# Spreading an expert's closing steps over two stages of the next expert

## The chip, the cores and the metric

The kernel runs on one core of a Trainium2 chip. The metric is the device time of one execution in microseconds (us). Three runs of the kernel before took between 1490.14 and 1492.38 us, with a median of 1491.45 us.

## The reference, cut to what matters

Two decoder layers on 256 tokens of width 1024, all in float32. The first layer ends in a dense SwiGLU, the second in eight SwiGLU experts of width 3584, of which each token takes two. The change is in the experts alone:

```python
def swiglu(x, w_gate, w_up, w_down):
    return (jax.nn.silu(x @ w_gate) * (x @ w_up)) @ w_down
...
y = y * w_buf[:, None].astype(y.dtype)
out = jax.ops.segment_sum(y, tok_buf, num_segments=T)
```

An expert's tokens are gathered, put through its three weight matrices, weighted by their gate and added back to the rows of the tokens that they came from.

## The kernel before, in words

`experts` (L980) works through eight jobs, one for each expert. The first is expert 0, the others come in a fixed order of their ranks by token count (`TURN`, L42). A job is **wide** (128 token slots) or **narrow** (64 slots); jobs 1, 3 and 5 are narrow. Each job runs in two chunks of 1792 hidden columns (c = 0 and 1), and each chunk in two stages, called gate and up here:

- **gate**: eight pieces of the gate weights (k = 0 to 7, L1169) come by DMA from SP's queue. ACT copies each half of a piece to a rounded high part `wh` (L177), DVE subtracts to get the low part `wl` (L180), and PE multiplies the gathered tokens `xg` by both (L1053). There are eight buffers for `wh` and eight for `wl`, so ACT and DVE can be at most eight halves ahead of PE. In a narrow job the eighth piece is multiplied as it came, without splitting.
- **up**: the same for the up weights (L1202). Before it ACT applies Silu to the gate's products (L1194); after it DVE multiplies the two (L1217).

The pieces of the down matrix of the chunk before are split and multiplied in between (`more`, `down`), some before the Silu, some behind the up pieces. A wide half costs PE six matmuls (four with `wh`, two with `wl`), a narrow one four, while ACT and DVE do the same work for both.

Around these loops a list `side` holds small steps. One step is taken behind each piece, and those left over run behind the last piece. Four kinds of step go on it:

- `to_features` (L1125): PE transposes the finished chunk, ACT and DVE split it into `hT`.
- `combine` (L1088): two parts for an expert whose last down product is done. Part i has ACT copy half i of the result out of PSUM into `ys` (L1092) and DVE make its low part (L1093); then, for two blocks of tokens, two matmuls with the one-hot matrix `DT` send the rows to their tokens and one DVE instruction adds them to `x_tok` (L1099).
- `transposed` (L1033): DVE writes a one-hot block `D` (L999), PE transposes it, DVE copies it to `DT` (L1040). It serves the combine of the same job later.
- `dispatch` (L1003): DVE writes the one-hot `D` of the next one or two jobs, at once; then eight steps, each with four matmuls into a PSUM bank of tag "a" and the ACT copies into `xg` (L1023).

`side` is taken in gate by the transposes, the two combine parts and `transposed`, all in chunk 1 of the next job. In up of chunk 1 of jobs 0, 2, 4 and 6 it is taken by the eight dispatch steps; in the other up stages it is empty. `D` and `ys` share one tag, "ys", whose pool has one buffer, so each of these tiles waits until the one before it has been read.

The order on each engine is laid down when the kernel is built, by a list scheduler: among the instructions whose inputs its own timing says are ready, it takes the one that comes first in the program. An instruction far down the program can therefore stand early on an engine that would otherwise be idle. `pin` keeps marked instructions in program order among themselves; `fence` keeps later `wl` behind a dispatch's `D`.

Of the kernel before, what the change touches and what calls it, by code (L numbers as in the profile page):

```python
# [9 lines left out]
F32 = mybir.dt.float32  # L10
F32R = mybir.dt.float32r
I32 = mybir.dt.int32
AF = mybir.ActivationFunctionType
ALU = mybir.AluOpType
# [3 lines left out]
P = 128  # L18
T = 256
NB = 2  # L20
D = 1024
# [44 lines left out]
def trunk(ctx, tc, x, positions, w_in, conv_w, a_log, dt_bias, gdn_norm_w, lam_q1, lam_k1, lam_q2, lam_k2,  # L66
# [3 lines left out]
    V, S, G, PE = nc.vector, nc.scalar, nc.gpsimd, nc.tensor  # L70
# [9 lines left out]
    def nm(s):  # L80
        cnt[0] += 1
        return f"{s}_{cnt[0]}"


    def bank(tag):
        return ps.tile([P, 512], F32, tag=tag, name=nm("ps_" + tag))
# [8 lines left out]
    def pin(ins):  # L95
        return tc.keep_in_program_order(ins)

    def mm(o, lhsT, rhs, start, stop):
        return PE.matmul(o, lhsT, rhs, start=start, stop=stop, skip_group_check=True)  # L99
# [880 lines left out]
    def experts(xs, jobs, mp, ring2, rest, first):  # L980
# [13 lines left out]
        def slots(Dt, job, twice=False):  # L994

            _, where, _, narrow = job
            w = 64 if narrow else P
            m = 2 if narrow and twice else 1
            return V.tensor_tensor(Dt.rearrange("p b (m s) -> p b m s", s=w),  # L999
                                   io1[:, 0:w].unsqueeze(1).unsqueeze(1).broadcast_to([P, NB, m, w]),  # L1000
                                   where.unsqueeze(3).broadcast_to([P, NB, m, w]), op=ALU.is_equal)

        def dispatch(group, early=False):  # L1003

            ws = [64 if job[3] else P for job in group]
            W = sum(ws)
            Dt = mp.tile([P, NB, W], F32R, tag="ys", name=nm("D"))
            for j, job in enumerate(group):
                fence[0] = pin(slots(Dt[:, :, sum(ws[:j]):sum(ws[:j + 1])], job))
            xgs = [xg_tile(job[3]) for job in group]  # L1010

            def part(k):
                pt = bank("ab"[k % 2] if early else "a")
                for c in range(2):
                    for b in range(NB):
                        mm(pt[:, c * W:(c + 1) * W], xs[b][:, c, k * P:(k + 1) * P], Dt[:, b], c == 0 and b == 0,
                           c == 1 and b == 1)
                for j, xg in enumerate(xgs):
                    i = pt[:, 0:2 * W].rearrange("p (c s) -> p c s", s=W)[:, :, sum(ws[:j]):sum(ws[:j + 1])]
                    if early and k % 2:  # L1020
                        fence[0] = pin(V.tensor_copy(xg[:, k], i))
                    else:
                        S.activation(xg[:, k], i, AF.Copy)  # L1023

            return xgs, [lambda k=k: part(k) for k in range(KD)]
# [5 lines left out]
            return x_  # L1031

        def transposed(n):  # L1033
            Dt = mp.tile([P, NB, P], F32R, tag="ys", name=nm("D"))
            slots(Dt, jobs[n], True)
            DT = mp.tile([P, NB, P], F32R, tag=f"DT{n % 2}", name=nm("DT"), bufs=1)
            pt = bank("a")
            for b in range(NB):
                PE.transpose(pt[:, b * P:(b + 1) * P], Dt[:, b].bitcast(F32), ident)
            V.tensor_copy(DT.rearrange("p b t -> p (b t)"), pt[:, 0:NB * P])  # L1040
            return DT
# [44 lines left out]
                                   k == K - 1 and w is wl)  # L1086

        def combine(n, py, DT):  # L1088
            def part(i):
                ys = mp.tile([P, 2, 512], F32R, tag="ys", name=nm("ys"))  # L1090
                yh, yl = ys[:, 0], ys[:, 1]
                S.activation(yh, py[i], AF.Copy)  # L1092
                V.tensor_tensor(yl, py[i], yh.bitcast(F32), op=ALU.subtract)  # L1093
                for b in range(NB):
                    pt = bank("a")
                    mm(pt, DT[:, b], yh, True, False)
                    mm(pt, DT[:, b], yl, False, True)
                    o = x_tok[:, b, i * 512:(i + 1) * 512]
                    V.scalar_tensor_tensor(o, pt, jobs[n][2][:, b], o, op0=ALU.mult, op1=ALU.add)  # L1099

            return [lambda i=i: part(i) for i in range(2)]

        regs = {}

# [39 lines left out]
        def gu_banks():  # L1144
            return [bank(t)[:, 0:BANK] for t in ("mm", "mm", "gd", "gd")]

        groups = [[0], [1, 2], [3, 4], [5, 6], [7]] if NARROW and rest else [[n] for n in range(NE)]
        pend = None
        side = []
        tiles, steps = dispatch([jobs[n] for n in groups[0]], True)  # L1150
        for step in steps:
            step()
        xgs = dict(zip(groups.pop(0), tiles))
        most = []
        if rest:
            side = [lambda: None, lambda: most.append(rest())]
        for n, job in enumerate(jobs):
            narrow = job[3]
            rows = slice(0, 64) if narrow else slice(0, P)
            xg = xgs.pop(n)  # L1160
            x32 = as_one(xg) if narrow else None
            wg, wu = (weights(n, i).rearrange("(k p) c -> p k c", p=P) for i in range(2))
            for c in range(NC):
                banks = gu_banks()
                for k, f in enumerate(first or ()):
                    products(banks, xg, narrow, k, f)
                downs = down_pieces(pend[0], pend[1]) if pend else iter(())
                subs, moves = None, ()
                for sub in in_pieces(wg, c, len(first or ()), narrow):  # L1169
                    if narrow and sub[0] == KD - 1:  # L1170
                        subs = next(downs, None)
                        moves = leads(banks)
                    products(banks, xg, narrow, *sub, x32)
                    if side and sub[0]:
                        side.pop(0)()
                first = None
                fence[0] = fence_high[0] = None
                while side:
                    side.pop(0)()
                hh = mp.tile([P, CHUNK], F32, tag="hh", name=nm("hh"))  # L1180
                if pend and not pend[3]:
                    pend[3].extend([bank("b"), bank("b")])

                def more(subs=None):
                    subs = subs or next(downs, None)
                    if subs:
                        down(subs, *pend)

                more(subs)
                for move in moves:  # L1190
                    move()
                more()
                for i, p in enumerate(banks):
                    pin(S.activation(hh[rows, i * BANK:(i + 1) * BANK], p[rows, :], AF.Silu))  # L1194
                more()
                banks = gu_banks()
                if c == NC - 1 and groups and n + 1 not in xgs:
                    group = groups.pop(0)
                    tiles, side = dispatch([jobs[g] for g in group])
                    xgs.update(zip(group, tiles))  # L1200
                subs, moves = None, ()
                for sub in in_pieces(wu, c, 0, narrow):  # L1202
                    if narrow and sub[0] == KD - 1:
                        subs = next(downs, None)
                        moves = leads(banks)
                    products(banks, xg, narrow, *sub, x32)
                    if side:
                        side.pop(0)()
                while side:
                    side.pop(0)()  # L1210
                more(subs)
                for move in moves:
                    move()
                more()
                for i, p in enumerate(banks):
                    h = hh[rows, i * BANK:(i + 1) * BANK]
                    pin(V.tensor_tensor(h, h, p[rows, :], op=ALU.mult))  # L1217
                for subs in downs:
                    down(subs, *pend)
                hT, side = to_features(hh, narrow)  # L1220
                if pend and pend[1] == NC - 1:
                    side += combine(pend[0], pend[3], DT)
                if c == 0:
                    py = []
                    later = []
                    side.append(lambda n=n, later=later: later.append(transposed(n)))
                else:
                    DT = later[0]
                pend = (n, c, hT, py)
# [16 lines left out]
        pt = bank("a")  # L1246
# [9 lines left out]
        ys = mp.tile([P, 2, 512], F32, tag="hh", name=nm("ys"))  # L1256
# [81 lines left out]
    with tc.tile_pool(name="rp", bufs=1) as rp:  # L1338
# [3 lines left out]
        pt = bank("a")  # L1342
# [7 lines left out]
        n = rp.tile([P, NB, 32], F32, name="turns")  # L1350
# [108 lines left out]
```

## Time and profile before

| | |
|---|---|
| median of three runs | 1491.45 us |
| the profiled execution | 1492.99 us |
| its span, first to last instruction | 1490.9 us |
| granted TensorE clock, mean | 0.988 |
| stretch of the experts | 521 to 1436 us |

The span is what the profile covers; the 2.1 us beyond it lie around the first and the last instruction. In every row a time is in us from the start of the span unless ns is written. PE are the matmuls, PEld their weight loads, DVE, ACT, POOL and SP the other engines. A pair of a narrow and a wide expert takes 230.5 us and comes three times, so the rows below are taken from one such pair: chunk 1 of job 1 (narrow), the two chunks of job 2 (wide), and chunk 0 of job 3 (narrow).

### The profile page before, as it was taken

The numbers are of one execution on the slowest core, as the hardware profiler recorded it, in microseconds if no ns is written. First come the engines' busy times: TensorE is split into PE (matmuls) and PEld (weight loads), VectorE is DVE, ScalarE is ACT, GpSimd is POOL, SyncE is SP. The second block draws the span as 40 slices with busy tenths as digits, with TensorE's granted clock in tenths as the row PEclk, the third lists the DMA queues.
The fourth block names the chain that finished last, engine by engine and source line by source line (L and its number), as shares of the span: only waits on it lengthen the run. The fifth ranks groups of instructions, "written<-read, shape, count | busy, mean of one in ns | idle before, by whom it ended". The sixth has DMA issues, their size and how long they took to land.

```text
span 1490.9 us, 24038 instructions
## 1 busy us (share of the span) xinstructions
PE 1448.6 (97%) x8873; PEld 1233.1 (83%) x8873; DVE 1218.3 (82%) x1609; ACT 1036.6 (70%) x1553; POOL 23.7 (2%) x37
## 2 busy tenths in 40 slices
PE   8999999999999999999999999999999999999995
PEld 8978899998987889886698877588877589888884
DVE  6877655556796798989899989899989899989886
ACT  5748544456666587787797887886887877778763
POOL 1100000000000000000000000000000000000000
PEclk9999999999999999999999999999999999999998
DMA  9633455535533179999999999999999899999891
GB/s 322 219 106 118 153 195 195 193 121 196 193 113 100 54 298 363 386 371 374 380 394 384 375 390 394 356 393 408 352 379 417 335 395 413 338 357 395 292 394 34
DMA packets 89124, 433.93 MB, mean 291 GB/s; under 512 B 7816, under 2 KB 9992, under 8 KB 74912
## 3 DMA queue, kind: packets, MB, share of 16 engines
q1 hardware_dynamic: 87808, 428.54, 76.1%
q0 software_dynamic: 1184, 3.71, 0.9%
q8 instruction: 73, 1.20, 0.3%
q14 instruction: 59, 0.48, 0.1%
HBM read 431.17 MB, written 1.05 MB: 290 GB/s over the span
## 4 chain that ended last, share of the span: by engine, by line
PE 87%; DVE 7%; issue 2%; ACT 2%; DMA 0%; DVEq 0%; SPq 0%; ACTq 0%
PE ps_b L99 26%; PE ps_mm L99 25%; PE ps_gd L99 24%; PE ps_a L99 9%; DVE wl L180 4%; PE ps_a L1137 2%; ACT wh L177 1%; DVE x_in L1099 1%; PE ps_mm L566 0%; ACT junk L415 0%; DVE hT L1140 0%; ACT xT L240 0%; PE ps_gd L408 0%; PE ps_mm L670 0%; DVE D L999 0%
## 5 line engine op out<-in xcount | busy, mean ns | idle before, releaser
L180 DVE TENSOR_TENSOR wl<-raw,wh 128x896 fp32r<-128x896 f32 (+2 forms) x851 | 925.7, 1144 | 145.8 <-ACT wh L177 139.4
L177 ACT ACTIVATE wh<-raw 128x896 fp32r<-128x896 f32 (+2 forms) x851 | 792.4, 995 | 153.4 <-PE ps_gd L99 68.4
L99 PE MATMUL ps_b<-wh,hT 128*128 128x512 f32 x816 | 232.6, 396 | 0.7 <-ACT hT L1139 0.7
L99 PE MATMUL ps_gd<-wh,xg 128*128 128x448 f32 x808 | 218.8, 368 | 0.0
L99 PE MATMUL ps_mm<-wh,xg 128*128 128x448 f32 x808 | 212.5, 372 | 0.3
L99 PEld LDWEIGHTS ps_b<-wh,hT 128*128 128x128 f32 x816 | 152.0, 188 | 39.2 <-issue 6.4
L99 PEld LDWEIGHTS ps_gd<-wh,xg 128*128 128x128 f32 x808 | 151.9, 189 | 12.7
L99 PE MATMUL ps_b<-wl,hT 128*128 128x512 f32 x492 | 159.0, 400 | 2.2 <-DVE wl L180 2.2
L99 PEld LDWEIGHTS ps_mm<-wh,xg 128*128 128x128 f32 x808 | 147.6, 189 | 16.4 <-ACT wh L177 2.0
L99 PE MATMUL ps_gd<-wl,xg 128*128 128x448 f32 x488 | 142.9, 374 | 8.9 <-DVE wl L180 7.2
L99 PE MATMUL ps_mm<-wl,xg 128*128 128x448 f32 x488 | 140.7, 369 | 0.1
L99 PEld LDWEIGHTS ps_b<-wl,hT 128*128 128x128 f32 x492 | 90.9, 188 | 31.9 <-DVE wl L180 6.7
L99 PEld LDWEIGHTS ps_gd<-wl,xg 128*128 128x128 f32 x488 | 88.8, 188 | 27.7 <-DVE wl L180 20.2
L99 PEld LDWEIGHTS ps_mm<-wl,xg 128*128 128x128 f32 x488 | 90.9, 188 | 11.7 <-DVE wl L180 4.3
L1139 ACT ACTIVATE hT<-ps_a 128x512 fp32r<-128x512 f32 (+2 forms) x52 | 27.4, 544 | 64.8 <-PE ps_a L1137 37.7
L99 PE MATMUL ps_mm<-xT,wh 128*128 128x256 f32 x448 | 70.9, 280 | 0.0
L99 PEld LDWEIGHTS ps_mm<-xT,wh 128*128 128x128 f32 x448 | 60.8, 189 | 0.4
L1140 DVE TENSOR_TENSOR hT<-ps_a,hT 128x512 fp32r<-128x512 f32 (+2 forms) x52 | 31.8, 621 | 26.5 <-ACT hT L1139 26.5
L99 PE MATMUL ps_gd<-xT,wh 128*128 128x256 f32 x320 | 50.5, 280 | 0.0
L1092 ACT ACTIVATE ys<-ps_b 128x512 fp32r<-128x512 f32 x14 | 8.4, 599 | 53.2 <-PE ps_b L99 39.0
L99 PE MATMUL ps_mm<-xT,wl 128*128 128x256 f32 x224 | 44.6, 280 | 0.0
L99 PEld LDWEIGHTS ps_gd<-xT,wh 128*128 128x128 f32 x320 | 43.1, 189 | 0.0
(407 smaller groups left out, 1660.2 us busy)
## 6 DMA issues: line engine op xcount, KB each, us to landing
raw<-in_moe_w_gate_dram SPq DMA_DIRECT2D x128, 896.0 KB, 8.2
raw<-in_moe_w_up_dram SPq DMA_DIRECT2D x128, 896.0 KB, 6.6
raw<-in_moe_w_down_dram SPq DMA_DIRECT2D x110, 1024.0 KB, 8.1
raw<-in_w_in_dram SPq DMA_DIRECT2D x24, 1024.0 KB, 6.6
raw<-in_ffn_w_gate_dram SPq DMA_DIRECT2D x11, 1024.0 KB, 5.1
raw<-in_ffn_w_up_dram SPq DMA_DIRECT2D x11, 1024.0 KB, 5.1
raw<-in_ffn_w_down_dram SPq DMA_DIRECT2D x11, 1024.0 KB, 4.9
raw<-in_w_out_dram SPq DMA_DIRECT2D x8, 1024.0 KB, 4.9
```

The lines of the kernel that those rows point to most:

```text
L99: return PE.matmul(o, lhsT, rhs, start=start, stop=stop, skip_group_check=True)
L177: high = S.activation(wh[:, c:c + n], w, AF.Copy)
L180: low = V.tensor_tensor(wl[:, c:c + n], w, wh[:, c:c + n].bitcast(F32), op=ALU.subtract)
L1092: S.activation(yh, py[i], AF.Copy)
L1099: V.scalar_tensor_tensor(o, pt, jobs[n][2][:, b], o, op0=ALU.mult, op1=ALU.add)
L1137: PE.transpose(pt[:, f * w:(f + 1) * w], hv[:, f0 + f], ident[rows, rows])
L1139: S.activation(hT[:, f0:f0 + n_, 0], pv, AF.Copy)
L1140: V.tensor_tensor(hT[:, f0:f0 + n_, 1], pv, hT[:, f0:f0 + n_, 0].bitcast(F32), op=ALU.subtract)
```

## The change

`combine` is cut in two. The copies out of PSUM stay on `side` and are taken in gate as before. The additions, with `transposed` behind them, go onto a new list, `carry`, which becomes `side` when up begins. The dispatch is now itself a step behind them: its one-hot `D` is written when that step is taken, and its eight steps follow. The tag "ys" gets two buffers.

```diff
-            Dt = mp.tile([P, NB, W], F32R, tag="ys", name=nm("D"))
+            Dt = mp.tile([P, NB, W], F32R, tag="ys", name=nm("D"), bufs=2)
...
-            Dt = mp.tile([P, NB, P], F32R, tag="ys", name=nm("D"))
+            Dt = mp.tile([P, NB, P], F32R, tag="ys", name=nm("D"), bufs=2)
...
         def combine(n, py, DT):
-            def part(i):
-                ys = mp.tile([P, 2, 512], F32R, tag="ys", name=nm("ys"))
-                yh, yl = ys[:, 0], ys[:, 1]
-                S.activation(yh, py[i], AF.Copy)
-                V.tensor_tensor(yl, py[i], yh.bitcast(F32), op=ALU.subtract)
+
+            parts = []
+
+            def copy(i):
+                ys = mp.tile([P, 2, 512], F32R, tag="ys", name=nm("ys"), bufs=2)
+                S.activation(ys[:, 0], py[i], AF.Copy)
+                V.tensor_tensor(ys[:, 1], py[i], ys[:, 0].bitcast(F32), op=ALU.subtract)
+                parts.append(ys)
+
+            def add(i):
                 for b in range(NB):
                     pt = bank("a")
-                    mm(pt, DT[:, b], yh, True, False)
-                    mm(pt, DT[:, b], yl, False, True)
+                    mm(pt, DT[:, b], parts[i][:, 0], True, False)
+                    mm(pt, DT[:, b], parts[i][:, 1], False, True)
                     o = x_tok[:, b, i * 512:(i + 1) * 512]
                     V.scalar_tensor_tensor(o, pt, jobs[n][2][:, b], o, op0=ALU.mult, op1=ALU.add)
 
-            return [lambda i=i: part(i) for i in range(2)]
+            return [lambda i=i: copy(i) for i in range(2)], [lambda i=i: add(i) for i in range(2)]
...
                 banks = gu_banks()
+                side, carry = carry, []
                 if c == NC - 1 and groups and n + 1 not in xgs:
-                    group = groups.pop(0)
-                    tiles, side = dispatch([jobs[g] for g in group])
-                    xgs.update(zip(group, tiles))
+                    def gather(group=groups.pop(0), side=side):
+                        tiles, steps = dispatch([jobs[g] for g in group])
+                        xgs.update(zip(group, tiles))
+                        side.extend(steps)
+
+                    side.append(gather)
...
                 if pend and pend[1] == NC - 1:
-                    side += combine(pend[0], pend[3], DT)
+                    copies, carry = combine(pend[0], pend[3], DT)
+                    side += copies
                 if c == 0:
                     py = []
                     later = []
-                    side.append(lambda n=n, later=later: later.append(transposed(n)))
+                    carry.append(lambda n=n, later=later: later.append(transposed(n)))
```

## Rows read from the trace of the kernel before

**Rows 1.** The page: busy time of each engine, and the chain that ended last.

```profile
PE 1448.6 (97%) x8873; PEld 1233.1 (83%) x8873; DVE 1218.3 (82%) x1609; ACT 1036.6 (70%) x1553; POOL 23.7 (2%) x37
...
PE 87%; DVE 7%; issue 2%; ACT 2%; DMA 0%; DVEq 0%; SPq 0%; ACTq 0%
```

**Rows 2.** Busy time by stage: narrow gate, up; wide chunk 0; wide gate, up; narrow chunk 0.

```profile
core 0: us, PE busy (x) PEld busy (x) DVE busy (x) ACT busy (x) POOL busy (x), PEclk, DMA share, GB/s
676.40:710.00 33.60, 31.55 (x136) 22.84 (x136) 30.35 (x36) 21.11 (x29) 0.00 (x0) 1.00 0.96 365
710.00:734.60 24.60, 23.72 (x93) 15.61 (x92) 21.02 (x20) 23.19 (x31) 0.00 (x0) 1.00 0.91 366
734.60:787.70 53.10, 53.10 (x257) 46.84 (x256) 50.49 (x52) 43.17 (x52) 0.00 (x0) 1.00 1.00 401
787.70:818.80 31.10, 31.10 (x154) 27.57 (x152) 29.10 (x36) 21.59 (x29) 0.00 (x0) 1.00 0.98 390
818.80:849.30 30.50, 29.94 (x157) 26.70 (x156) 28.89 (x31) 24.96 (x42) 0.00 (x0) 1.00 0.96 360
849.30:906.90 57.60, 57.34 (x257) 44.61 (x255) 51.13 (x53) 48.73 (x64) 0.00 (x0) 1.00 1.00 395
```

**Rows 3.** Waits, narrow gate (676.4:710): who waited for whom, us, times, longest.

```profile
PEld ps_gd L99 <- DVE wl L180: 2.6, 2, 1.6
...
PEld ps_mm L99 <- DVE wl L180: 0.9, 2, 0.5
```

**Rows 4.** Waits, narrow up (710:734.6).

```profile
PEld ps_gd L99 <- DVE wl L180: 3.4, 7, 0.7
```

**Rows 5.** Waits, wide up (818.8:849.3).

```profile
PEld ps_b L99 <- DVE wl L180: 1.0, 2, 0.8
```

**Rows 6.** Timeline of DVE, narrow gate and up: start, length, instruction, idle before.

```profile
694.40 1.41 DVE L1099 SCALAR_TENSOR_TENSOR x_in<-ps_a,route,x_in 128x512 f32<-128x512 f32 x2
...
698.32 1.40 DVE L1099 SCALAR_TENSOR_TENSOR x_in<-ps_a,route,x_in 128x512 f32<-128x512 f32 x2
...
700.63 0.42 DVE L999 TENSOR_TENSOR D<-io,sorted 128x256 fp32r<-128x256 f32 x1
...
701.97 0.42 DVE L1040 CAST DT<-ps_a 128x256 fp32r<-128x256 f32 x1
...
712.76 17.53 DVE L180 TENSOR_TENSOR wl<-raw,wh 128x1024 fp32r<-128x1024 f32 x17 [3.23 <-ACT wh L177]
```

**Rows 7.** Timeline of ACT, narrow gate and up.

```profile
684.83 0.60 ACT L1092 ACTIVATE ys<-ps_b 128x512 fp32r<-128x512 f32 x1 [4.80 <-PE ps_b L99]
...
709.96 0.97 ACT L1194 ACTIVATE hh<-ps_mm 64x448 f32<-64x448 f32 x2 [2.07 <-PE ps_mm L99]
```

**Rows 8.** Timeline of DVE, end of the wide gate.

```profile
812.82 0.75 DVE L1099 SCALAR_TENSOR_TENSOR x_in<-ps_a,sorted,x_in 128x512 f32<-128x512 f32 x1 [0.58 <-PE ps_a L99]
...
816.38 1.41 DVE L1099 SCALAR_TENSOR_TENSOR x_in<-ps_a,sorted,x_in 128x512 f32<-128x512 f32 x2 [0.21 <-PE ps_a L99]
```

**Rows 9.** Groups by form, 520:1440: count | busy us, mean ns | idle before, releasers.

```profile
L180 DVE TENSOR_TENSOR wl<-raw,wh 128x896 fp32r<-128x896 f32 x488 | 499.6, 1087 | 21.5 <-ACT wh L177 19.2
...
L99 PE MATMUL ps_a<-ys,DT 128*128 128x512 f32 x56 | 17.9, 395 | 0.0
...
L1099 DVE SCALAR_TENSOR_TENSOR x_in<-ps_a,sorted,x_in 128x512 f32<-128x512 f32 x24 | 17.2, 747 | 3.4 <-PE ps_a L99 3.4
...
L1093 DVE TENSOR_TENSOR ys<-ps_b,ys 128x512 fp32r<-128x512 f32 x14 | 9.6, 686 | 6.5 <-ACT ys L1092 6.5
...
L1092 ACT ACTIVATE ys<-ps_b 128x512 fp32r<-128x512 f32 x14 | 8.4, 599 | 53.2 <-PE ps_b L99 39.0 <-PE ps_a L99 14.2
```

**Rows 10.** Timeline of ACT, wide up: two dispatch steps and the work between.

```profile
845.37 0.55 ACT L1023 ACTIVATE xg<-ps_a 128x128 fp32r<-128x128 f32 x2 [0.29 <-PE ps_a L99]
845.81 2.01 ACT L177 ACTIVATE wh<-raw 128x1024 fp32r<-128x1024 f32 x2
848.25 0.55 ACT L1023 ACTIVATE xg<-ps_a 128x128 fp32r<-128x128 f32 x2 [0.44 <-PE ps_a L99]
```

More of the change, by code (lines that the diff above doesn't have):

```diff
@@ L1149, in experts @@
         side = []
+        carry = []
         tiles, steps = dispatch([jobs[n] for n in groups[0]], True)
```

## The prediction

> **What bounds the kernel now.** I start at the page. PE is busy for 97% of the span and makes up 87% of the chain that ended last, DVE 7% [rows 1]. The reader is to see that only time in which PE starves can be won, and that DVE is the engine most often behind it. An average says nothing of where, so next comes busy time by stage [rows 2]. In the wide chunk 0 PE has no idle time (53.10 of 53.10), in the wide gate none either (31.10 of 31.10). In the narrow gate it lacks 2.05 us (33.60 - 31.55), in the narrow up 0.88, in the wide up 0.56. The waits say for what: PE's weight loads wait on `wl` for 2.6 and 0.9 us in the narrow gate [rows 3], 3.4 in the narrow up [rows 4] and 1.0 in the wide up [rows 5]. The timeline of DVE then shows why. In the second half of the narrow gate the additions (1.41 and 1.40), the one-hot block (0.42) and its copy (0.42) stand between the `wl` subtractions [rows 6]. A narrow half costs PE four matmuls and DVE a full 1.09 us [rows 9], so DVE has no reserve there. In the narrow up DVE is busy 21.02 of 24.60 us [rows 2], and most of the rest is one pause of 3.23 [rows 6], in which ACT sits behind the Silu and the Silu waits for PE (2.07 idle) [rows 7]. Busy time and pause come to 24.25 of 24.60: the narrow up is paced by DVE from end to end. The wide stages are paced by PE, except where DVE comes late out of gate.
>
> **The change, part by part.** No instruction is removed or added; they move. Nothing that moves issues a DMA, and POOL has no work here (0.00 in every stage [rows 2]). SP issues the same loads in the same order, each when a `wl` frees its buffer, so an earlier DVE means earlier loads.
>
> *Narrow gate, three times.* DVE loses 1.41 + 1.40 + 0.42 + 0.42 = 3.65 us [rows 6]. As DVE sets the pace from the first addition to the end of this gate, it becomes shorter by that amount; PE, which loses eight matmuls (17.9 us for 56 [rows 9], so at most 0.32 each and 2.6 together), doesn't bind first: it lost at least 2.05 us to waits besides. Gain 3.65.
>
> *Narrow up, three times.* The same 3.65 us of DVE arrive where DVE is full. If they stand behind the first pieces, as the text of the program has it, up becomes longer by 3.65 and nothing is won. But the scheduler pulls ready work into idle time: ACT's copy out of PSUM belongs behind the piece k = 3 and stands ahead of a whole gate, at 684.83 [rows 7]. The additions will be ready from the middle of gate, since the copies are done there, `DT` is one chunk old and two buffers of "ys" no longer make copy 1 wait for addition 0. So I expect their matmuls in PE's gaps, and the additions themselves in DVE's pause. It holds 3.23 us; one pair fits (1.41); the second (1.40) needs the two PSUM banks that the first frees, a round trip of the kind that cost 0.58 in the wide gate [rows 8]. Bounds of what is hidden: above, the whole pause, 3.23; below, nothing, and even two round trips of 0.58 more on DVE, so -1.2. I take 2.1, the middle between one pair (1.41) and two (2.81), because the row of the pause is the nearest. Net for a narrow expert 3.65 - 3.65 + 2.1 = 2.1; three times, 6.3.
>
> *Wide gate and up, four times (jobs 2, 4, 6, 7; job 0 has no combine).* The wide gate is PE's, so taking 3.65 us from DVE there saves nothing inside it. But DVE leaves it late: its last additions start at 816.38, after a wait of 0.21 [rows 8], and the first down pieces of up wait for `wl` 1.0 us by the weight loads [rows 5] or 0.56 by PE's idle time [rows 2]. With the additions gone DVE is some 3 us earlier at that point, and the wait goes: 0.75, the middle of the two, with 0 and 1.0 as bounds. Against that stands copy 1, which no longer waits for a buffer and comes right behind copy 0: its 0.69 us of DVE [rows 9] fall at the start of gate, where DVE has just waited for ACT. Bounds 0 and 0.69, taken 0.35. In up DVE then carries 28.89 + 3.65 = 32.5 us against PE's 29.94 + 2.6 = 32.5: level, so I put the additions there at nothing; their cover is the reserve that DVE brings from gate, and without it each of the two pairs would cost PE at most its 1.41 us of DVE. Net 0.4; four times, 1.6.
>
> *The dispatch.* Its `D` is written at k = 3, four of its steps follow at k = 4 to 7, four behind the last piece. The tokens are needed only in the next job's gate, behind four down pieces, so I cost the delay at nothing; if the cover is gone, the rival below applies. The new waits are `D` on addition 1 and `transposed` on addition 0 (two buffers): queued behind them on DVE are `wl` halves, and PE waits for those; the matmuls in question are by then two pieces old, so nothing.
>
> *Transfers.* Over the pair DMA was unused for 33.6 x 0.04 + 24.6 x 0.09 + 31.1 x 0.02 + 30.5 x 0.04 = 5.4 us [rows 2]. The pair is to be 2.5 us shorter with the same bytes. Wide chunk 0 already stands at 1.00, so part of what the narrow stages win may come back there: bounds 0 and 2.1 a pair, taken 0.45, nearer to 0 because loads are issued by DVE's progress and more than twice the gain is unused. Three times, -1.4.
>
> *Sum.* 6.3 + 1.6 - 1.4 = 6.5 us. The profiled execution took 1492.99 us (span 1490.9), so it would take 1486.5; the median lies 1.54 below it, so I predict 1485.0.
>
> A page speaks against any gain. The Trainium skill ("DMA: Bandwidth & Descriptors", Where 436 GB/s comes from) says that loads from HBM are held to some 358 GB/s per core; another ("Perfetto Trace Analysis", Roofline) lets a core that runs alone reach about 435. The trace contradicts the first and allows the second: 401 and 395 GB/s over whole stages [rows 2].
>
> **The rivals.**
>
> *The additions stay in the full part of up.* The scheduler's timing may see no idle DVE there, or it may put the additions back into gate ahead of `wl`, so that the change undoes itself. For it: in gate the additions stood where the program has them, between `wl` halves [rows 6]. Against it: the early copy [rows 7]. Then the narrow experts give 0 and only the 1.6 of the wide ones remain: 1489.9; with the extra round trips, 3 x 1.2 = 3.5 more: 1493.4.
>
> *The transfers take it back.* DMA is at 1.00 in half of the pair [rows 2], and if its idle time in the narrow stages is the lag between a freed buffer and the load, it doesn't shrink; the pair keeps its length: 1491.5. Against it: 5.4 us unused. The first page above would have it so.
>
> *Slower: the late dispatch steps.* Four steps behind the last piece share two PSUM banks. The seventh needs the bank of the fifth, the eighth that of the sixth. ACT empties one step every 2.88 us, because two `wh` of 2.01 together stand between (848.25 - 845.37) [rows 10]. If PE's order holds the four steps together and ACT's keeps its `wh` between, PE waits for the seventh until the fifth's copies (0.55) are done, and for the eighth one round of ACT longer, 2.88, of which I estimate that some 0.8 pass with the matmuls and copies of the seventh: 0.55 + 2.1, or 2.6 us, four times 10.4, and 1485.0 becomes 1495.4. Against it: the scheduler knows the banks and has four pieces of down matmuls to put between. It decides the sign from 1.6 us a dispatch (6.5 / 4).
>
> **How the numbers follow.** A measurement of this kernel can tell about 0.2%, 3 us, from no change. Forecast 0.57 (faster; its own range runs from 1478.0, with the whole pause used and nothing taken back: 3 x 3.2 + 4 x 0.75 = 12.7, to 1488.4); additions in the full part 0.15 (same); transfers 0.11 (same); dispatch 0.17 (slower). So faster 0.57, same 0.26, slower 0.17. The range 1478.0 to 1495.0 holds all but the worse half of the last rival and the best tail of the first case.
>
> **What would show it.** Right: in the narrow gate the additions are gone from between the `wl` rows and the gate is about 30 us instead of 33.6; in the narrow up DVE's pause before `wl` is mostly filled with additions, and up is 26 to 27 us; in the wide up the weight loads' wait of 1.0 on `wl` is gone; ACT's wait for PE before copy 1 is gone (14.2 us in all [rows 9]); DMA's share in the narrow stages rises. Wrong: the pause of 3.23 still there and additions behind it, with up near 28 us; PE waiting for ACT's `xg` copies behind the up pieces; DMA releasing `wh` in the wide gate. If PE's idle time in the narrow gate stays at 2 us, my reading that DVE paces it by the additions is wrong.

## The result, and the profile after

The changed kernel took a median of 1500.02 us (1497.14 to 1502.07, four runs) against 1491.18 for the kernel before (four runs): a ratio of 1.0064, 95% interval 1.005 to 1.0077. It is slower, by 0.6%, and lies 5 us above the predicted range. The profiled execution took 1497.14 us, its span is 1495.0, its mean granted clock 0.988 as before.

The page of the changed kernel: busy time, and the chain that ended last.

```profile
PE 1448.5 (97%) x8873; PEld 1232.2 (82%) x8873; DVE 1218.4 (82%) x1609; ACT 1037.0 (69%) x1553; POOL 23.7 (2%) x37
...
PE 85%; DVE 7%; ACT 4%; issue 3%; DMA 0%; DVEq 0%; SPq 0%; ACTq 0%
```

The same work [rows 1], while PE's part of the chain falls from 87% to 85% and ACT's rises from 2% to 4%. Where that sits, busy time by stage shows: the stages of [rows 2] in the changed kernel, in the same order.

```profile
678.10:711.70 33.60, 31.01 (x136) 22.98 (x136) 30.33 (x36) 20.98 (x29) 0.00 (x0) 1.00 0.95 374
711.70:736.30 24.60, 23.70 (x93) 15.60 (x92) 21.02 (x20) 23.19 (x31) 0.00 (x0) 1.00 0.88 353
736.30:789.40 53.10, 53.10 (x257) 46.75 (x256) 50.43 (x51) 42.96 (x52) 0.00 (x0) 1.00 1.00 400
789.40:819.40 30.00, 30.00 (x148) 26.54 (x147) 28.19 (x34) 21.62 (x28) 0.00 (x0) 1.00 0.98 385
819.40:853.00 33.60, 32.85 (x168) 28.90 (x166) 29.62 (x32) 24.62 (x37) 0.00 (x0) 1.00 0.99 368
853.00:909.90 56.90, 56.08 (x250) 43.40 (x249) 51.36 (x54) 49.34 (x68) 0.00 (x0) 1.00 0.97 384
```

The narrow gate is as long as before, to the tenth (33.60), and so is the narrow up (24.60). The wide gate is 1.1 shorter, the wide up 3.1 longer, the narrow chunk 0 behind it 0.7 shorter: 1.3 us lost for the pair. All pairs and single stages of the experts, compared one by one, add up to about 3.5 us lost in this execution. The other terms of the 4.1 us between the two spans are the start of the experts, 2.5 us later though the programs are the same up to there, the first gate of expert 0, 1.2 shorter (its granted clock was 1.00 here and 0.93 before), and the end behind the experts, 0.7 shorter.

**The additions went back into gate.** The timeline of DVE, narrow gate and up of the changed kernel, answers [rows 6].

```profile
697.08 0.75 DVE L1104 SCALAR_TENSOR_TENSOR x_in<-ps_a,route,x_in 128x512 f32<-128x512 f32 x1
...
699.74 0.74 DVE L1104 SCALAR_TENSOR_TENSOR x_in<-ps_a,route,x_in 128x512 f32<-128x512 f32 x1
...
702.41 1.40 DVE L1104 SCALAR_TENSOR_TENSOR x_in<-ps_a,route,x_in 128x512 f32<-128x512 f32 x2
703.73 0.41 DVE L999 TENSOR_TENSOR D<-io,sorted 128x256 fp32r<-128x256 f32 x1
704.67 0.42 DVE L1040 CAST DT<-ps_a 128x256 fp32r<-128x256 f32 x1 [0.53 <-PE ps_a L1039]
...
714.47 17.52 DVE L180 TENSOR_TENSOR wl<-raw,wh 128x1024 fp32r<-128x1024 f32 x17 [3.70 <-ACT wh L177]
```

Gate ends at 711.7. Four additions, the one-hot block and its copy stand ahead of that as before. Counted from the start of gate they come 1.0 to 3.0 us later, the additions by 1.0, 3.0, 2.4 and 2.4, the block by 1.4 and its copy by 1.0. The pause that they were to fill is still there (3.70). The waits of the same gate, beside [rows 3]:

```profile
PEld ps_b L99 <- DVE wl L180: 1.6, 1, 1.6
PEld ps_a L1039 <- DVE D L999: 1.4, 1, 1.4
PEld ps_gd L99 <- DVE wl L180: 1.2, 2, 0.7
```

PE now also waits for `D` itself, which it did not before. Its idle time in the gate rose from 2.05 to 2.59 us (33.60 - 31.01).

**The last dispatch steps wait for banks.** The timeline of PE at the end of the wide up (the one-hot products of the dispatch alone), and that of ACT over the same time:

```profile
850.33 1.03 PE L99 MATMUL ps_a<-D,xs 128*128 128x192 f32 x8
...
851.95 1.14 PE L99 MATMUL ps_a<-D,xs 128*128 128x192 f32 x8 [0.34 <-ACT xg L1023]
853.78 0.69 PE L99 MATMUL ps_a<-D,xs 128*128 128x192 f32 x4 [0.69 <-ACT xg L1023]
```

```profile
851.35 0.99 ACT L1023 ACTIVATE xg<-ps_a 128x128 fp32r<-128x128 f32 x4
852.19 1.10 ACT L177 ACTIVATE wh<-raw 128x1024 fp32r<-128x1024 f32 x1
853.14 0.58 ACT L1023 ACTIVATE xg<-ps_a 128x128 fp32r<-128x128 f32 x2
```

Five steps stand side by side on PE behind the last piece (8 + 8 + 4 matmuls, with a single down matmul between), and PE waits twice for ACT to empty a bank, 1.03 us in all. It is the rival of the late dispatch steps, but ACT puts one `wh` (1.10) between two copies and not two (2.01 in [rows 10]), so the two waits come to less than the 2.6 worked out there. Of [rows 5], the wait for `wl` in the wide up went from 1.0 to 0.8 and not to nothing:

```profile
PEld ps_b L99 <- DVE wl L180: 0.8, 1, 0.8
PEld ps_a L99 <- ACT xg L1023: 0.6, 1, 0.6
```

### The profile page after: what moved, and what is told of

Its sections match the earlier page's. It is cut to its first block, busy times and chain, and to the rows that moved or that the text cites. A ratio compares the mean times of both kernels' runs of the same rounds, so it can differ in the third digit from the quotient of the medians.

```text
span 1495.0 us, 24052 instructions
## 1 busy us (share of the span) xinstructions
PE 1448.5 (97%) x8873; PEld 1232.2 (82%) x8873; DVE 1218.4 (82%) x1609; ACT 1037.0 (69%) x1553; POOL 23.7 (2%) x37
## 4 chain that ended last, share of the span: by engine, by line
PE 85%; DVE 7%; ACT 4%; issue 3%; DMA 0%; DVEq 0%; SPq 0%; ACTq 0%
PE ps_b L99 25%; PE ps_mm L99 25%; PE ps_gd L99 24%; PE ps_a L99 9%; DVE wl L180 5%; ACT wh L177 2%; PE ps_a L1142 2%; DVE x_in L1104 1%; PE ps_mm L566 0%; ACT xg L1023 0%; ACT junk L415 0%; ACT xT L240 0%; ACT hT L1144 0%; PE ps_gd L408 0%; PE ps_mm L670 0%
## 5 line engine op out<-in xcount | busy, mean ns | idle before, releaser
L99 PE MATMUL ps_mm<-wh,xg 128*128 128x448 f32 x808 | 209.5, 370 | 0.0
L1023 ACT ACTIVATE xg<-ps_a 128x256 fp32r<-128x256 f32 (+1 forms) x60 | 17.8, 355 | 31.0 <-PE ps_a L99 31.0
```

## The experiments

The first theory: the scheduler put the additions back, so the narrow experts give nothing, and the late dispatch makes the loss. Against it stood that the additions, wherever they are, or the two buffers cost the time. A third cause came up on the way, and the later runs are about it. All times below stand against runs of the kernel before on the same chip in the same hour.

| kernel | median, us | before, us | ratio, 95% interval | mean granted clock of its runs (of those of before) |
|---|---|---|---|---|
| again | 1497.80 | 1491.97 | 1.0043, 1.0027 to 1.006 | 0.988 (0.990) |
| late_dispatch | 1495.29 | 1491.97 | 1.002, 1.0006 to 1.0034 | 0.991 (0.990) |
| two_steps | 1497.32 | 1491.97 | 1.0036, 1.0021 to 1.005 | 0.987 (0.990) |
| two_buffers | 1490.65 | 1491.97 | 0.9987, 0.9974 to 1.0001 | 0.991 (0.990) |
| held_two | 1484.68 | 1491.64 | 0.9944, 0.9922 to 0.9966 | 0.991 (0.990) |
| gate_end | 1482.11 | 1491.64 | 0.9929, 0.9903 to 0.9955 | 0.990 (0.990) |
| late_block | 1496.35 | 1491.64 | 1.0028, 1.0013 to 1.0042 | 0.988 (0.990) |
| d_held | 1490.42 | 1492.12 | 0.9991, 0.9975 to 1.0007 | 0.990 (0.990) |

### The changed kernel twice more (again, again_b), and the kernel before twice more (before_a, before_b)

> The changed kernel once more. Its first profile has the experts' stretch about 3.6 us longer than before, while the medians differ by 8.8. Theory A (the change costs what that profile shows, and the rest is TensorE's clock in stretches that the change doesn't touch): the experts' stretch is again 3 to 4.5 us longer, and what is left of the difference lies ahead of it or in stretches at 1.2 GHz. Theory B (the change costs some 8 us in the experts, and the first profile was a lucky one): the stretch is 7 to 9 us longer in this profile.

The loss is confirmed, 5.8 us. But this profile differs from the first of the same kernel: the experts take 922.0 us and not 915.9. Busy time in its three narrow gates (columns as in [rows 2]):

```profile
676.31:711.62 35.31, 32.70 (x135) 23.39 (x135) 30.38 (x36) 21.01 (x29) 0.00 (x0) 0.95 0.96 372
909.70:946.40 36.70, 34.08 (x135) 23.71 (x135) 30.39 (x36) 21.02 (x28) 0.00 (x0) 0.91 0.93 360
1145.11:1180.17 35.06, 32.44 (x135) 23.38 (x135) 30.39 (x36) 21.02 (x28) 0.00 (x0) 0.95 0.95 372
```

The granted clock is 0.95, 0.91 and 0.95 in stages where it was 1.00, so part of each ran at 1.2 GHz, the lower level, and the gates are 1.7, 3.1 and 1.4 us longer. The timeline of PE shows where, and what PE did before:

```profile
702.45 0.44 PE L1039 MATMUL ps_a<-cst,D 128*128 128x128 f32 x2 [0.97 <-DVE D L999]
...
704.54 0.50 PE L99 MATMUL ps_b<-wl,hT 128*128 128x512 f32 x1 [1.18 <-DVE wl L180]
704.97 2.85 PE L99 MATMUL ps_mm<-raw,xg 128*64 128x448 f32 x4
707.61 2.28 PE L99 MATMUL ps_gd<-raw,xg 128*64 128x448 f32 x4
```

After the waits for `D` (0.97) and `wl` (1.18) the eight unsplit products take 2.85 and 2.28 us. In the first profile of the changed kernel, behind the same two waits (0.98 and 1.17), they took 1.72 and 1.67, as in the kernel before:

```profile
706.71 1.72 PE L99 MATMUL ps_mm<-raw,xg 128*64 128x448 f32 x4
708.26 1.67 PE L99 MATMUL ps_gd<-raw,xg 128*64 128x448 f32 x4
```

The difference, 1.74, is what that gate lost (35.31 - 33.62 = 1.69). The experts' stretch, 8.5 us above that of before (913.5), is as long as theory B has it. But its cause is the clock, and that in stages that the change does touch: neither theory had named this.

> The changed kernel once more, one look. K and L both: one to three half-clock stretches inside the narrow gates, each 1.5 to 3.1 us longer, and an experts' stretch of 917 to 922 us; all other stages within 0.1 us of the first profile of the changed kernel (so 915.9 us if the clock holds).

In two of three gates the clock fell (36.49 us at 0.91 and 35.21 at 0.95; the third took 33.62 at 1.00), and the experts took 921.4 us, as expected.

> The kernel before, unchanged: one more look at whether the granted TensorE clock also falls to 1.2 GHz inside its narrow gates. Theory K (the fall belongs to the placement of the closing steps in the changed kernel): none inside the experts in this profile, narrow gates 33.6 us, as in the first profile of before. Theory L (it can fall in any execution of any of these kernels, and only its frequency differs): a half-clock stretch of 3.4 or 6.8 us in one of the three narrow gates in this look or its twin, and that gate 1.5 to 3.1 us longer. Two looks can show L, they cannot exclude it.

> The twin of the look above, with the same expectations: K no half-clock stretch inside the experts, L one in a narrow gate, which is then 1.5 to 3.1 us longer.

The clock fell in no narrow gate of either; this is the first of them in before_a:

```profile
675.08:708.70 33.62, 31.61 (x135) 22.81 (x135) 30.38 (x36) 21.12 (x29) 0.00 (x0) 1.00 0.96 360
```

The experts took 913.5 and 913.6 us, as in the first profile (913.5). So there are three profiles of before without a fall in a narrow gate, and of three of the changed kernel two with falls, which cost 6.2 us (35.31 + 36.70 + 35.06 less three times 33.62) and 4.5 us. That is what K expects; that it needs the changed placement, as K has it, late_block below contradicts. With the 3.5 us of the stages, the three profiles give 3.5 + (0 + 6.2 + 4.5) / 3 = 7.1 us; measured were 5.8 and 8.8.

### The late dispatch alone (late_dispatch)

The kernel before, with its dispatch taken as a step some pieces later:

```diff
-                    group = groups.pop(0)
-                    tiles, side = dispatch([jobs[g] for g in group])
-                    xgs.update(zip(group, tiles))
+                    def gather(group=groups.pop(0), side=side):
+                        tiles, steps = dispatch([jobs[g] for g in group])
+                        xgs.update(zip(group, tiles))
+                        side.extend(steps)
+
+                    side.extend([lambda: None] * (3 if n else 1) + [gather])
```

> The kernel before with the dispatch alone moved: its one-hot block is written and its steps begin three pieces later (one for job 0), the combine as before. Theory A (PE waits for PSUM banks behind the last up piece, 1.4 us a dispatch, and ACT is held in front of its first copy): 3 to 6 us slower than before, with the two waits on ACT's xg copies after the last piece in jobs 2 and 4. Rival C (the loss is in the divided combine with its two buffers): same as before within 1.5 us.

3.3 us slower, as theory A has it, with no fall of the clock in a narrow gate. Its wide up and the timeline of PE there:

```profile
816.86:849.48 32.62, 31.73 (x163) 27.94 (x161) 28.70 (x30) 24.40 (x38) 0.00 (x0) 1.00 0.95 358
```

```profile
848.42 1.14 PE L99 MATMUL ps_a<-D,xs 128*128 128x192 f32 x8 [0.34 <-ACT xg L1023]
850.25 0.69 PE L99 MATMUL ps_a<-D,xs 128*128 128x192 f32 x4 [0.69 <-ACT xg L1023]
```

The same two bank waits, 0.34 and 0.69. The up is 2.1 us longer than 30.5 [rows 2] and the chunk behind it 0.8 shorter; the four dispatches lose 0.45, 1.34, 1.39 and 0.57 us, 3.75 in all. That is the whole of the 3.5 us that the changed kernel loses by stages.

### Two dispatch steps behind each of the last pieces (two_steps)

```diff
-                        side.extend(steps)
+                        side.extend(lambda s=steps[i:i + 2]: [t() for t in s] for i in range(0, KD, 2))
```

> The changed kernel with two dispatch steps behind each of the pieces k = 4 to 7, so that none is left behind the last piece. Theory A: the waits for banks behind the last piece go, the time falls back to within 2 us of before. Rival C: it stays 6 to 9 us above before. A third way: the waits move in among the pieces, because two steps still share two banks with ACT's queue, and half of the loss stays.

None of the three came out. The bank waits are gone, as the timeline of PE shows (no idle time before the last two):

```profile
849.26 1.03 PE L99 MATMUL ps_a<-D,xs 128*128 128x192 f32 x8
...
852.58 1.30 PE L99 MATMUL ps_a<-D,xs 128*128 128x192 f32 x8
```

Wide gate, up and the next gate of the pair (-1.15, +3.17, -2.12) now add up to nothing against before. Yet the time stays, 5.4 us above it, for in this profile the clock fell in all three narrow gates:

```profile
677.46:712.64 35.18, 32.57 (x135) 23.43 (x135) 30.38 (x36) 21.01 (x29) 0.00 (x0) 0.95 0.96 371
909.51:944.72 35.21, 32.59 (x135) 23.43 (x135) 30.39 (x36) 21.02 (x29) 0.00 (x0) 0.95 0.95 371
1142.08:1178.74 36.66, 34.06 (x135) 23.71 (x135) 30.38 (x36) 21.02 (x28) 0.00 (x0) 0.91 0.93 359
```

They are 1.6, 1.6 and 3.0 us longer than at full clock (33.62), 6.2 in all. From the first Silu of the experts to DVE's last product of gate and up, this profile takes 6.1 us more than before (894.8 in place of 888.7). So without the falls nothing is left of the loss in it: spreading the dispatch steps removes the 3.5 us of the stages, and the rest is the clock.

### Two buffers alone (two_buffers)

The kernel before, with `bufs=2` on its three tiles of the tag "ys".

> The kernel before with two buffers for the tag ys and nothing else. Theory A: same as before within 1.5 us (copy 1 comes earlier, the additions stay where they were). Rival C: 3 to 8 us slower, since copy 1 and its subtraction then stand ahead of wl halves at the start of gate.

Its first narrow gate:

```profile
676.87:709.88 33.01, 31.21 (x135) 22.92 (x135) 30.38 (x36) 20.99 (x28) 0.00 (x0) 1.00 0.97 372
```

0.6 us shorter in each narrow gate, and 1.3 us in the medians, which is within the noise (the interval holds 1). The buffers are not the loss.

### The additions kept out of gate (held_two)

two_steps, and an ordering edge that costs nothing at run time: the first matmul of each addition may not stand ahead of the last down matmul before the Silu (`after[0]`, set there).

```diff
                     pt = bank("a")
-                    mm(pt, DT[:, b], parts[i][:, 0], True, False)
+                    order(mm(pt, DT[:, b], parts[i][:, 0], True, False), after[0])
```

> The kernel two_steps with one more edge: the matmuls of the additions may not be scheduled ahead of the last down matmul before the Silu, so that the additions really stand in up. It asks what the step of the prediction would have given if the scheduler had not pulled the additions back. Theory A (DVE paces the narrow gate by the additions, and the clock falls there because PE waits long at its end): the narrow gate is 3 to 4 us shorter (30 instead of 33.6), the narrow up 2 to 4 us longer, no stretch at 1.2 GHz inside the experts; the time is within 3 us of before and some 5 us below two_steps. Rival D (the narrow gate is paced by something else, such as ACT behind the transposes): the narrow gate stays above 32.5 us.

7 us faster than before, where theory A had it within 3 us. Narrow gate and up:

```profile
677.42:707.13 29.71, 29.24 (x125) 21.26 (x125) 27.23 (x31) 21.85 (x29) 0.00 (x0) 1.00 1.00 402
...
707.13:733.97 26.84, 25.71 (x103) 17.37 (x102) 24.27 (x27) 22.25 (x30) 0.00 (x0) 1.00 0.99 389
```

With the additions really gone, the gate is 3.9 us shorter (predicted 3.65) and the up 2.2 longer. PE's idle time in the gate falls from 2.05 to 0.47 us, so the premise of the prediction holds: DVE sets this gate's pace by the additions. But that is 1.6 of the 3.9 us; the other 2.3 are PE's own work, which moved to up with them (31.5 to 29.24). With the additions out PE paces the gate, so that 3.9 lies so near 3.65 is in part chance. DMA follows, from 0.96 to 1.00 in the gate, at 402 GB/s, and the wide chunk 0 behind it keeps its 53.1 us: the transfers take nothing back. The Trainium skill ("DMA: Bandwidth & Descriptors", Where 436 GB/s comes from) would hold a core to some 358 GB/s. By it the bytes of this gate would take an estimated 33.4 us (29.71 x 402 / 358), as long as the gate before; the measurement decides against it.

### The additions in DVE's pause (gate_end)

two_steps, with the narrow jobs' additions taken ahead of the Silu and their first matmuls ordered behind the last unsplit product of gate (`after[0]` there).

```diff
                 while side:
                     side.pop(0)()
+                while narrow and len(carry) > 1:
+                    carry.pop(0)()
```

> The kernel two_steps with the additions of the narrow jobs placed behind the last product of gate and kept from going earlier, so that they stand beside DVE's pause at the Silu. Theory A: narrow gate 3 to 3.6 us shorter, narrow up at most 1.5 us longer, because DVE works in the 3.2 to 3.7 us in which it waited for ACT; 5 to 9 us faster than before. Rival E (the pause can't be used, since it only moves behind the additions): gate shorter, up longer by the same, within 2 us of before.

9.5 us faster than the kernel before, the fastest of all. The timeline of DVE around the end of its narrow gate (708.66), then the two stages:

```profile
703.16 2.36 DVE L180 TENSOR_TENSOR wl<-raw,wh 128x1024 fp32r<-128x1024 f32 x2 [0.66 <-ACT wh L177]
705.76 1.41 DVE L1106 SCALAR_TENSOR_TENSOR x_in<-ps_a,route,x_in 128x512 f32<-128x512 f32 x2 [0.24 <-PE ps_a L99]
707.09 1.22 DVE L180 TENSOR_TENSOR wl<-raw,wh 128x1024 fp32r<-128x1024 f32 x1
708.22 1.40 DVE L1106 SCALAR_TENSOR_TENSOR x_in<-ps_a,route,x_in 128x512 f32<-128x512 f32 x2
709.54 3.22 DVE L180 TENSOR_TENSOR wl<-raw,wh 128x1024 fp32r<-128x1024 f32 x3
```

```profile
677.10:708.66 31.56, 31.08 (x133) 22.74 (x133) 28.84 (x33) 22.68 (x31) 0.00 (x0) 1.00 1.00 395
...
708.66:732.03 23.37, 23.00 (x95) 16.19 (x94) 22.57 (x25) 21.43 (x29) 0.00 (x0) 1.00 0.95 378
```

Both pairs stand at the Silu, with one wait of 0.24, and the long pause is gone. Gate and up are 2.0 and 1.3 us shorter, 3.3 for each narrow expert and 9.9 for three, more than the 2.1 each that the prediction counted. The parts came out otherwise than theory A had them (the gate 3 to 3.6 shorter, the up longer by at most 1.5). The matmuls of the additions stay in this gate, and PE fills it (31.08 of 31.56).

### What makes the clock fall: a later one-hot block (late_block), and its transposes kept out (d_held)

late_block is the kernel before, and narrow jobs write `D` three times (0.84 us more of DVE):

```diff
-            slots(Dt, jobs[n], True)
+            for _ in range(3 if jobs[n][3] else 1):
+                slots(Dt, jobs[n], True)
```

> The kernel before, with the one-hot block of the narrow jobs written three times (0.84 us more of DVE), so that PE's transposes wait for it in the narrow gate; nothing else moves. It adds to the narrow gate the kind of wait that the changed kernel has there. Theory A (in the changed kernel the granted clock falls because PE waits for D and for wl close together at the end of the narrow gate): the gate is 0.8 us longer, and in some executions TensorE goes to 1.2 GHz there, which costs 1.5 to 3 us each time; the time is 3 to 8 us above before. Rival F (the drops of the clock in the narrow gates have to do with the code of the changed kernel as a whole): 2.5 us above before, and no stretch at 1.2 GHz in the narrow gates.

4.7 us slower, but not by a longer gate or a new wait: two of its three narrow gates are as before, and the third is not.

```profile
675.94:709.51 33.57, 31.34 (x135) 22.83 (x135) 30.50 (x38) 21.10 (x28) 0.00 (x0) 1.00 0.93 354
...
1137.62:1174.22 36.60, 34.34 (x135) 24.01 (x135) 31.05 (x38) 21.10 (x29) 0.00 (x0) 0.91 0.92 347
```

The mean clock of its twelve runs is 0.9875 against 0.9903. So the fall does not need the moved steps, and rival F, which excluded it here, is wrong. That 0.84 us more of DVE are enough to bring it rests on this one gate and on the mean clock.

d_held is two_steps, where in narrow jobs the transposes of `D` stay behind the last product of gate, so that PE does not wait for `D` in it:

```diff
-                PE.transpose(pt[:, b * P:(b + 1) * P], Dt[:, b].bitcast(F32), ident)
+                t = PE.transpose(pt[:, b * P:(b + 1) * P], Dt[:, b].bitcast(F32), ident)
+                if jobs[n][3]:
+                    order(t, after[0])
```

> The kernel two_steps with one more edit: in narrow jobs the transposes of the one-hot block stay behind the last product of gate; the additions stay where the scheduler puts them. Theory M (PE's wait of 1.4 us for D in the narrow gate is what makes the clock fall more often): that wait is gone, the narrow gates are at or below 33.6 us, no half-clock stretch there, mean granted clock back to 0.990 to 0.991, and the time 3 to 6 us below two_steps, ratio to before 0.996 to 1.000. Rival N (what counts is DVE's load of additions among the wl halves, whichever step PE waits for): the clock still falls in one to three narrow gates, mean granted clock 0.986 to 0.988, ratio 1.002 to 1.005.

The time came as M has it: ratio 0.9991, mean clock 0.990, and a median 6.9 us below that of two_steps. But its profiled execution, at 0.988 one of the lower of its runs (0.986 to 0.994), shows the clock fallen in all three narrow gates, which M excludes. The first of them, and PE in it:

```profile
673.79:708.09 34.30, 32.19 (x133) 23.26 (x133) 29.95 (x35) 21.01 (x29) 0.00 (x0) 0.95 0.98 384
```

```profile
701.07 0.64 PE L99 MATMUL ps_b<-wl,hT 128*128 128x512 f32 x1 [1.66 <-DVE wl L180]
701.64 3.21 PE L99 MATMUL ps_mm<-raw,xg 128*64 128x448 f32 x4
```

One wait of 1.66 for `wl` stands there in place of the two, and the first four products behind it take 3.21 us in place of 1.72. At that price three falls cost 4.5 us; gate and up are only 1.0 us longer than before, so at full clock they would be some 0.5 shorter, or 1.5 for three narrow experts. The clock thus accounts for an estimated 5.4 of the 6.9 us. What is shown: without the wait for `D` the mean clock over twelve runs is as high as before. What is not shown: that this wait is the cause, or which waits decide. PE's idle time in the narrow gate is 2.59 us in the changed kernel, 2.23 in late_block and 2.11 in d_held, where the clock fell; 2.05 in before, 1.80 in two_buffers and 0.5 in held_two and gate_end, where it did not in any profile. That order fits idle time in general as the cause, but d_held and before lie too close together to settle it.

## Why the prediction was wrong

**Narrow gate, three times.** The step that failed. It said that DVE loses 3.65 us there. The weighing of "But the scheduler pulls ready work into idle time" was right, and applied to one place only: the additions were to be pulled forward out of up into the pause. Ready from the middle of gate, they were pulled further, back inside gate, where they had come from; PE's idle time there rose from 2.05 to 2.59 us. It was the rival *the additions stay in the full part of up*, in its second form ("so that the change undoes itself"), at 0.15. The argument against it, the early copy of [rows 7], spoke for it. held_two shows that the placement decided: kept out by an edge, the gate is 3.9 us shorter. The clause that PE "doesn't bind first" was wrong there: with the additions out PE is busy for 29.24 of 29.71 us.

**Narrow up, three times.** The 2.1 us hidden in the pause did not come, since nothing arrived there; the pause stayed, at 3.70. gate_end shows that the pause holds both pairs with one round trip of 0.24, so its true value lay at the upper bound, 3.2, and not at 2.1.

**Wide gate and up.** Forecast a gain of 0.4 for each. The wait for `wl` went from 1.0 only to 0.8, because an addition stands there too (on DVE at 820.05, 0.75 us). two_steps, which has this part without the bank waits, gives 0.1 a pair: worth nothing, near the lower bound of the 0.75, which was 0.

**The dispatch.** The step "so I cost the delay at nothing" failed too: late_dispatch measures 3.75 us for four, 0.45 to 1.39 each, where the rival had 2.6. Its place and its banks were right; ACT's round was taken with two `wh` between and has one. With the gain of the narrow experts gone, that was enough to decide the sign.

**Transfers.** The 1.4 was not called on, as the pair did not get shorter. Where it did, in held_two, nothing came back (wide chunk 0 took 53.11 us against 53.08).

**The range.** Its lower end does not follow from its own sum: 1491.45 - 12.7 is 1478.8 and not 1478.0. As the miss is at the other end, nothing hangs on it.

**What no step named** is the clock. About half of the loss, 3.6 of the 7.1 us that three profiles give, is a granted clock of 0.91 to 0.95 in the narrow gates of some executions, at 1.4 to 3.1 us a gate. The waits of [rows 3] were counted at their own length, and a wait on PE can cost more than that. The Trainium skill ("TensorE: Matmul & The Clock Gate", HAM oscillation — how this bites in real kernels) tells of PE falling to half rate when each tile ends in a wait for data that is longer than the tile's own work. The rows agree only in that the fall comes right behind waits: these are of 0.7 to 1.7 us, in a stage that PE fills to 92%. Why it comes in some executions of one kernel and not in others stays open.

## What to carry to other kernels

Under a list scheduler, a step moved in the program's text is not yet moved on the engines: ask where its inputs become ready, expect it there, and where the place matters fix it by an ordering edge (here the difference between the ratios of two_steps, 1.0036, and held_two, 0.9944). Steps that share two banks cost 0.45 to 1.39 us a dispatch here when left to the end, and nothing that could be measured when spread by twos between other work. And one profile does not show a loss that comes in only some executions: compare the mean granted clocks of all runs before giving the difference to a stage. That mean counts the whole program, so a single one says little: the three profiles of before have 0.988, 0.991 and 0.991, and in none of them did the clock fall in a narrow gate.

## What the runs showed of the hardware that was not expected

TensorE's clock fell to its lower level inside stages that PE fills to over 90%, behind the same waits, in two of three profiles of one program, and in none of three of another whose idle time there is half a microsecond less (2.05 against 2.59 us). The eight unsplit products behind such a wait took 5.13 us in place of 3.39. With 2.11 us of idle time, in d_held, the clock fell in all three narrow gates of the one profile.
